# Attention over running maxima with the row sums in the value matmul, and its preparation with joint statistics

## The chip, the core and the metric

The kernel runs on one core of a Trainium2 chip. Its engines work side by side, each through its own list of instructions in order: TensorE (PE; PEld is its weight load), VectorE (DVE), ScalarE (ACT), GpSimd (POOL), and SyncE (SP), which issues the transfers. They meet at semaphores. The metric is the time of one execution on the device in microseconds.

## The reference

One inference step of a model of two layers, for 256 prompt tokens and 2048 latent tokens. Each layer projects the normalised input once into the inputs of four mixers (latent attention, a long convolution called Hyena, a state space called S5, gated linear attention called GLA), gates their outputs and projects them once back. The change touches the attention branch:

```
c_q = rmsnorm(c_q, p['mla_qa_norm'])
c_kv = rmsnorm(c_kv, p['mla_kva_norm'])
q = rmsnorm((c_q @ p['mla_w_uq']).reshape(b, L, MLA_HEADS, MLA_QK), p['mla_q_norm'])
k, v = mla_keys_values(c_kv, k_rope, p)
...
s = jnp.einsum('bqhd,bkhd->bhqk', qi, k).astype(jnp.float32) * (MLA_QK ** -0.5)
pr = jax.nn.softmax(s, axis=-1).astype(v.dtype)
return jnp.einsum('bhqk,bkhd->bqhd', pr, v)
```

There are 4 heads of 96 (64 of them from the latent, 32 rotary) with values of 64. A latent query reads 512 cached and 2048 latent keys; a prompt query reads the 256 prompt keys.

## The kernel before

Per layer the work runs in stages. First the input projection (`inproj`, its matmuls are in `mm3`, L268 to L270) with, beside it, S5 and the preparation of the attention (`mla_prep`). Then the attention for heads 0 and 1, with Hyena and GLA beside it. Then the attention for heads 2 and 3 with the output projection (L1817 to L1819). A scheduler that goes by priorities and by its own model of durations lays out each engine's list; the program text only gives the priorities.

`mla_prep` goes over 22 tiles of 128 tokens, 18 of this step and 4 cached. For a tile it computes the mean squares of c_q and c_kv, takes the inverse root with a helper of 13 VectorE instructions (`rsqrt`, an integer first guess and three Newton steps), scales, transposes, multiplies with the up-projections, takes a second inverse root for the 8 head vectors (4 of q, 4 of k), scales each, turns the rotary part on GpSimd (`rotate`), splits the result into two f16 halves (`split`) and stores it through a transposing transfer. Values are stored as high half in columns 0 to 63 and low half in 64 to 127.

`attention` goes over units, one head and one tile of 128 queries. A latent unit has three chunks of keys (1024, 1024 and 512), so there are 128 such units in the two layers, and 16 prompt units of one chunk. `scores` makes the scores of a chunk in PSUM in parts of 512 with three f16 matmuls each (L485 to L487), takes each part's row maximum (m, L488), the chunk's maximum (L492), from it the bias nb of the exponential (L493), and lets ScalarE write the exponentials e with their row sums su (L495). `values` splits e into f16 halves ph (L508 or L510, and L511 on GpSimd), turns them with a transposing transfer into pt (L513), and multiplies with V into one PSUM tile om (L517, L518). `combine` weighs the chunks against each other with al and the sums su, adds them up and writes the head's output o (L528 to L540). The scores of one chunk are issued ahead of the values of the chunk before. There is one buffer for om.

## Time and profile before

| | us |
|---|---|
| median of the 3 runs (lowest 4432.41, highest 4437.69) | 4437.48 |
| the profiled execution | 4438.93 |
| its span, first to last instruction | 4436.9 |
| TensorE busy in the span | 3680.0 |
| VectorE busy | 3222.7 |
| ScalarE busy | 2175.1 |
| GpSimd busy | 2048.8 |

Busy times are sums over the whole span; the stages differ, so what a change in one of them is worth is read from that stage. The mean granted clock of TensorE is 0.897 of its full speed.

### The profile page before, as it was taken

The numbers are of one execution on the slowest core, as the hardware profiler recorded it, in microseconds if no ns is written. First come the engines' busy times: TensorE is split into PE (matmuls) and PEld (weight loads), VectorE is DVE, ScalarE is ACT, GpSimd is POOL, SyncE is SP. The second block draws the span as 40 slices with busy tenths as digits, with TensorE's granted clock in tenths as the row PEclk, the third lists the DMA queues.
The fourth block names the chain that finished last, engine by engine and source line by source line (L and its number), as shares of the span: only waits on it lengthen the run. The fifth ranks groups of instructions, "written<-read, shape, count | busy, mean of one in ns | idle before, by whom it ended". The sixth has DMA issues, their size and how long they took to land. (4 is left out here: it accounts for less than half of the span.)

```text
span 4436.9 us, 67211 instructions
## 1 busy us (share of the span) xinstructions
PE 3680.0 (83%) x21852; PEld 2141.3 (48%) x21852; DVE 3222.7 (73%) x8340; ACT 2175.1 (49%) x4333; POOL 2048.8 (46%) x2025
## 2 busy tenths in 40 slices
PE   6899889787877887769887688889998888667898
PEld 2644545343555555424443554545565555434444
DVE  4775589984788887776786678866548887767774
ACT  3533334556545564675453344363435555545563
POOL 2553354741555654654453244424325555434553
PEclk7999999898777887989998899999998888887999
DMA  7746657656776788998988565633448776999886
GB/s 207 193 122 182 175 146 191 188 155 221 168 172 150 173 186 212 239 235 203 250 192 203 148 156 145 154 111 123 145 156 193 184 168 157 210 246 240 173 185 157
DMA packets 1343430, 799.91 MB, mean 180 GB/s; under 512 B 989588, under 2 KB 1221296, under 8 KB 1341544
## 3 DMA queue, kind: packets, MB, share of 16 engines
q1 hardware_dynamic: 1343080, 795.63, 71.8%
q8 instruction: 173, 2.83, 0.3%
q14 instruction: 177, 1.45, 0.1%
HBM read 352.12 MB, written 207.37 MB: 126 GB/s over the span
## 5 line engine op out<-in xcount | busy, mean ns | idle before, releaser
L511 POOL TENSOR_TENSOR ph<-e,ph 128x1024 f16<-128x1024 f32 (+2 forms) x400 | 725.5, 1821 | 650.4 <-ACT ph L508 323.9
L495 ACT ACTIVATE e<-sp,nb,ssc 128x512 f32<-128x512 f32 (+1 forms) x656 | 499.9, 767 | 415.7 <-DVE nb L493 347.0
L488 DVE TENSOR_REDUCE m<-sp 128x1 f32<-128x512 f32 (+1 forms) x656 | 438.0, 676 | 172.0 <-PE sp L487 170.2
L268 PE MATMUL mm<-hT,ws 128*128 128x512 f16 (+1 forms) x1440 | 526.5, 366 | 26.2 <-DVE wqh L75 13.3
L269 PE MATMUL mm<-hT,ws 128*128 128x512 f16 (+1 forms) x1440 | 526.4, 366 | 0.0
L270 PE MATMUL mm<-hT,ws 128*128 128x512 f16 (+1 forms) x1440 | 525.8, 365 | 0.0
L517 PE MATMUL om<-V,pt 128*128 128x128 f16 x2560 | 303.8, 235 | 132.1 <-DMA pt<-ph 90.6
L485 PE MATMUL sp<-KT,qt 128*128 128x512 f16 x640 | 271.5, 424 | 102.5 <-ACT e L495 99.1
L517 PEld LDWEIGHTS <-pt 128*128 128x128 f16 x2592 | 258.9, 109 | 171.6 <-DMA pt<-ph 125.1
L508 ACT CAST ph<-e 128x1024 f16<-128x1024 f32 (+2 forms) x268 | 269.0, 1004 | 117.3 <-DMA pt<-ph 115.2
L518 PE MATMUL om<-V,pt 128*128 128x64 f16 x2560 | 293.7, 206 | 0.0
L518 PEld LDWEIGHTS <-pt 128*128 128x128 f16 x2592 | 248.2, 105 | 71.6 <-issue 58.5
L486 PE MATMUL sp<-KT,qt 128*128 128x512 f16 x640 | 271.4, 424 | 0.0
L487 PE MATMUL sp<-KT,qt 128*128 128x512 f16 x640 | 268.9, 420 | 0.0
L1606 PE MATMUL lv<-qh,kh 32*128 32x128 f32 x1440 | 227.7, 324 | 25.1 <-DVE m L492 10.2
L1606 PEld LDWEIGHTS lv<-qh,kh 32*128 32x128 f32 x1440 | 188.0, 218 | 98.8 <-issue 30.3
L1817 PE MATMUL mm<-wo,bh 128*128 128x512 f16 x576 | 223.7, 389 | 7.7 <-DVE oy L1820 6.7
L268 PE MATMUL mm<-ws,hT 128*128 128x256 f16 (+1 forms) x864 | 215.4, 264 | 15.8 <-ACT z L1688 13.4
L269 PEld LDWEIGHTS <-ws 128*128 128x128 f16 x1440 | 143.8, 100 | 175.2 <-issue 49.4
L1818 PE MATMUL mm<-wo,bh 128*128 128x512 f16 x576 | 224.1, 389 | 4.2 <-DVE wo L1772 4.2
L1819 PE MATMUL mm<-wo,bh 128*128 128x512 f16 x576 | 223.9, 389 | 2.8 <-DVE bh L1792 2.8
L268 PEld LDWEIGHTS <-ws 128*128 128x128 f16 x1440 | 143.9, 100 | 150.9 <-issue 26.1
(522 smaller groups left out, 9489.1 us busy)
## 6 DMA issues: line engine op xcount, KB each, us to landing
kab<-KS SPq DMA_DIRECT2D x128, 256.0 KB
wf<-in_w_in SPq DMA_DIRECT2D x22, 1024.0 KB
b<-br SPq DMA_DIRECT2D x36, 512.0 KB
A1F<-a SPq DMA_DIRECT2D x64, 256.0 KB
zg<-z SPq DMA_DIRECT2D x64, 256.0 KB
...
```

The source lines that it names most:

```text
L268: nc.tensor.matmul(ps, lhsT=lh, rhs=rh, start=i == 0, stop=False)
L269: nc.tensor.matmul(ps, lhsT=lh, rhs=rl, start=False, stop=False)
L270: nc.tensor.matmul(ps, lhsT=ll, rhs=rh, start=False, stop=i == n - 1)
L485: nc.tensor.matmul(d, lhsT=qh, rhs=kh, start=True, stop=False)
L486: nc.tensor.matmul(d, lhsT=qh, rhs=kl, start=False, stop=False)
L488: nc.vector.tensor_reduce(m[:, 2 * c + i:2 * c + i + 1], d, axis=AX.X, op=ALU.max)
L495: nc.scalar.activation(e[:, i * 512:min(i * 512 + 512, n)], d, AF.Exp, bias=nb[:, c:c + 1], scale=ssc, accum_out=su[:, 2 * c + i:2 * c + i ...
L508: nc.scalar.copy(ph[:, 0:n], e)
L511: nc.gpsimd.tensor_tensor(out=ph[:, n:2 * n], in0=e, in1=ph[:, 0:n], op=ALU.subtract)
L517: nc.tensor.matmul(om[:, c], lhsT=pt[:, i], rhs=v, start=i == 0, stop=False)
L518: nc.tensor.matmul(om[:, c, 0:64], lhsT=pt[:, nk + i], rhs=v[:, 0:64], start=False, stop=i == nk - 1)
L1606: nc.tensor.matmul(ps[:, cc], lhsT=kh[hh, cc], rhs=qh[hh, cc], start=True, stop=True, tile_position=(32 * h, 0))
```

## The change

In the attention the chunk's maximum becomes a running one: the new L492 reduces over all parts so far, so the third bias is the smallest and no minimum has to be found. The bias itself (L493) is made on ScalarE. V gets a column of ones (a memset on GpSimd) and its halves change places, low first; the second matmul of each pair takes columns 64 to 128, so that column 128 of om collects the row sum from both halves of the exponentials, and the accumulator su goes. `combine` copies the first chunk out of om on ScalarE, adds the other two on VectorE, takes one reciprocal from column 128 and applies it in two steps, one on ScalarE and one on VectorE.

In the preparation the mean squares of c_q and c_kv are made when the input projection is evacuated (`tm` in `inproj`, into the tile zst that also holds the ones for `total`), and their inverse roots are taken for six tiles at once. q and k of a tile lie in one tile W of eight heads, copied there from PSUM by ScalarE; one square, one reduce, one inverse root, eight scalings, one rotation over eight heads. The two f16 tiles for the split are made once, with their zero columns. `rsqrt` itself takes 11 instructions, 8 where it has one column. A pad of 48 columns is added to the pool of K and V.

```diff
-    v = pool.tile([128, n], F32, tag=tag + "v", name=tag + "v")
     t = pool.tile([128, n], F32, tag=tag + "t", name=tag + "t")
     w = pool.tile([128, n], F32, tag=tag + "w", name=tag + "w")
-    nc.vector.tensor_scalar(out=v, in0=x, scalar1=mul, scalar2=EPS, op0=ALU.mult, op1=ALU.add)
-    nc.vector.tensor_single_scalar(out=t.bitcast(I32), in_=v.bitcast(I32), scalar=1, op=ALU.logical_shift_right)
-    nc.vector.tensor_scalar(out=out.bitcast(I32), in0=t.bitcast(I32), scalar1=-1.0, scalar2=float(0x5F3759DF),
-                            op0=ALU.mult, op1=ALU.add)
-    nc.vector.tensor_scalar(out=w, in0=v, scalar1=-0.5, scalar2=None, op0=ALU.mult)
+
+    nc.vector.tensor_scalar(out=w, in0=x, scalar1=-0.5 * mul, scalar2=-0.5 * EPS, op0=ALU.mult, op1=ALU.add)
+    nc.vector.tensor_scalar(out=out.bitcast(I32), in0=w.bitcast(I32), scalar1=-0.5,
+                            scalar2=float(0x5F3759DF - (1 << 30) - (1 << 22)), op0=ALU.mult, op1=ALU.add)
     for _ in range(3):
-        nc.vector.tensor_tensor(out=t, in0=out, in1=out, op=ALU.mult)
-        nc.vector.tensor_tensor(out=t, in0=t, in1=w, op=ALU.mult)
+        if n == 1:
+            nc.vector.scalar_tensor_tensor(out=t, in0=out, scalar=out, in1=w, op0=ALU.mult, op1=ALU.mult)
+        else:
+            nc.vector.tensor_tensor(out=t, in0=out, in1=out, op=ALU.mult)
+            nc.vector.tensor_tensor(out=t, in0=t, in1=w, op=ALU.mult)
         nc.vector.scalar_tensor_tensor(out=out, in0=t, scalar=1.5, in1=out, op0=ALU.add, op1=ALU.mult)
...
     def rotate(x, rope):
...
-        cs = rope[:, 0].unsqueeze(1).to_broadcast([128, 4, 32])
+        cs = rope[:, 0].unsqueeze(1).to_broadcast([128, 8, 32])
...
-    def split(x, dst, tag):
-
-        hl = tp.tile([128, NH, 2, 128], F16, tag=tag, name=tag, bufs=2)
+
+    hls = [tp.tile([128, NH, 2, 128], F16, name=f"hl{i}", bufs=1) for i in range(2)]
+    for hl in hls:
         nc.gpsimd.memset(hl[:, :, :, 96:128], 0.0)
+
+    def split(i, x, dst):
+
+        hl = hls[i]
         nc.scalar.copy(hl[:, :, 0, 0:96], x)
         nc.vector.tensor_tensor(out=hl[:, :, 1, 0:96], in0=x, in1=hl[:, :, 0, 0:96], op=ALU.subtract)
...
+    RS = 6
     for t in range(22):
         isctx = t >= 18
+        h0 = 4 if isctx else 0
         if not isctx:
+            if t % RS == 0:
+                rs = tp.tile([128, RS, 2], F32, tag="rs", name="rs", bufs=2)
+                rsqrt(s, tp, rs.rearrange("p t c -> p (t c)"), s.zst[:, t:t + RS].rearrange("p t c -> p (t c)"), 1.0, 2 * RS, "cr")
             z = tp.tile([128, 384], F32, tag="z", name="z", bufs=2)
             nc.sync.dma_start(z, s.zm[l][t * 128:(t + 1) * 128])
             kr = z[:, 320:352]
             if t < 16:
                 rope = tp.tile([128, 2, 32], F32, tag="rope", name="rope", bufs=2)
                 nc.sync.dma_start(rope, I["k_rope"][:, t])
-            st = tp.tile([128, 2], F32, tag="st", name="st")
-            rs = tp.tile([128, 2], F32, tag="rs", name="rs")
-            cn = tp.tile([128, 320], F32, tag="cn", name="cn")
-            nc.scalar.activation(cn[:, 0:192], z[:, 0:192], AF.Square, scale=192 ** -0.5, accum_out=st[:, 0:1])
-            nc.scalar.activation(cn[:, 192:320], z[:, 192:320], AF.Square, scale=128 ** -0.5, accum_out=st[:, 1:2])
-            rsqrt(s, tp, rs, st, 1.0, 2, "cr")
-            nc.vector.scalar_tensor_tensor(out=cn[:, 0:192], in0=z[:, 0:192], scalar=rs[:, 0:1], in1=qa, op0=ALU.mult, op1=ALU.mult)
-            nc.vector.scalar_tensor_tensor(out=cn[:, 192:320], in0=z[:, 192:320], scalar=rs[:, 1:2], in1=kva, op0=ALU.mult, op1=ALU.mult)
+            cn = tp.tile([128, 320], F32, tag="cn", name="cn", bufs=2)
+            nc.vector.scalar_tensor_tensor(out=cn[:, 0:192], in0=z[:, 0:192], scalar=rs[:, t % RS, 0:1], in1=qa, op0=ALU.mult, op1=ALU.mult)
+            nc.vector.scalar_tensor_tensor(out=cn[:, 192:320], in0=z[:, 192:320], scalar=rs[:, t % RS, 1:2], in1=kva, op0=ALU.mult, op1=ALU.mult)
             ckv = cn[:, 192:320]
...
+        W = tp.tile([128, 8, 96], F32, tag="qk", name="qk", bufs=2)
+        ct = tp.tile([128, 3, 128], F32, tag="ct", name="ct", bufs=2)
...
+        nc.scalar.copy(W[:, 4:8, 0:64], kv[:, :, 0:64])
+        nc.scalar.copy(W[:, 4:8, 64:96], kr.unsqueeze(1).to_broadcast([128, 4, 32]))
...
-            nc.scalar.activation(q2[:, 0:384], qp, AF.Square)
-            nc.vector.tensor_reduce(ss[:, 0:4], q2[:, 0:384].rearrange("p (h n) -> p h n", h=4), axis=AX.X, op=ALU.add)
-            rsqrt(s, tp, rr, ss, 1.0 / QK, 8, "qr")
-            q = tp.tile([128, 4, 96], F32, tag="qk", name="q")
-            for h in range(4):
-                nc.vector.scalar_tensor_tensor(out=q[:, h], in0=qp[:, h * 96:(h + 1) * 96], scalar=rr[:, h:h + 1], in1=qn,
-                                               op0=ALU.mult, op1=ALU.mult)
-            if t < 16:
-                rotate(q, rope)
-            split(q, s.QT[l][t].rearrange("p h a t -> p (h a) t"), "hl")
...
-        k = tp.tile([128, 4, 96], F32, tag="qk", name="k")
-        for h in range(4):
-            nc.vector.scalar_tensor_tensor(out=k[:, h, 0:64], in0=kv[:, h, 0:64], scalar=rr[:, 4 + h:5 + h], in1=kn[:, 0:64],
-                                           op0=ALU.mult, op1=ALU.mult)
...
+            nc.scalar.copy(W[:, 0:4], qp.rearrange("p (h n) -> p h n", h=4))
...
+        nh = 8 - h0
+        ss = tp.tile([128, nh], F32, tag=f"ss{nh}", name="ss", bufs=2)
+        rr = tp.tile([128, nh], F32, tag=f"rr{nh}", name="rr", bufs=2)
+        sq = tp.tile([128, 768], F32, tag="sq", name="sq", bufs=1).rearrange("p (h n) -> p h n", h=8)[:, h0:]
+        nc.scalar.activation(sq, W[:, h0:], AF.Square)
+        nc.vector.tensor_reduce(ss, sq, axis=AX.X, op=ALU.add)
+        rsqrt(s, tp, rr, ss, 1.0 / QK, nh, f"qr{nh}")
+        for h in range(h0, 8):
+            nc.vector.scalar_tensor_tensor(out=W[:, h], in0=W[:, h], scalar=rr[:, h - h0:h - h0 + 1], in1=qn if h < 4 else kn,
                                            op0=ALU.mult, op1=ALU.mult)
         if t < 16:
-            rotate(k, rope)
-        split(k, s.KT[l].rearrange("p h a t -> p (h a) t")[:, :, kt * 128:(kt + 1) * 128], "hl")
+            rotate(W, rope)
...
+            V = kp.tile([128, (b - a) // 128, 130], F16, tag="V" + nm, name="V" + nm)
             nc.sync.dma_start(K, s.KT[l][:, h, :, a:b])
-            nc.sync.dma_start(V, s.V[l][h, :, a // 128:b // 128])
+            nc.gpsimd.memset(V[:, :, 128:129], 1.0)
+            nc.sync.dma_start(V[:, :, 0:128], s.V[l][h, :, a // 128:b // 128])
...
-        mc = m[:, 2 * c:2 * c + 1]
-        if len(sps) > 1:
-            nc.vector.tensor_tensor(out=mc, in0=mc, in1=m[:, 2 * c + 1:2 * c + 2], op=ALU.max)
-        nc.vector.tensor_scalar(out=nb[:, c:c + 1], in0=mc, scalar1=nssc, scalar2=LN2_15, op0=ALU.mult, op1=ALU.add)
+        mc, k = m[:, 0:1], 2 * c + len(sps)
+        if k > 1:
+            mc = m[:, 5 + c:6 + c]
+            nc.vector.tensor_reduce(mc, m[:, 0:k], axis=AX.X, op=ALU.max)
+        nc.scalar.activation(nb[:, c:c + 1], mc, AF.Copy, scale=nssc, bias=LN2_15)
         for i, d in enumerate(sps):
-            nc.scalar.activation(e[:, i * 512:min(i * 512 + 512, n)], d, AF.Exp, bias=nb[:, c:c + 1], scale=ssc,
-                                 accum_out=su[:, 2 * c + i:2 * c + i + 1])
+            nc.scalar.activation(e[:, i * 512:min(i * 512 + 512, n)], d, AF.Exp, bias=nb[:, c:c + 1], scale=ssc)
...
-            nc.tensor.matmul(om[:, c], lhsT=pt[:, i], rhs=v, start=i == 0, stop=False)
-            nc.tensor.matmul(om[:, c, 0:64], lhsT=pt[:, nk + i], rhs=v[:, 0:64], start=False, stop=i == nk - 1)
+            nc.tensor.matmul(om[:, c], lhsT=pt[:, i], rhs=v[:, 0:129], start=i == 0, stop=False)
+            nc.tensor.matmul(om[:, c, 64:129], lhsT=pt[:, nk + i], rhs=v[:, 64:129], start=False, stop=i == nk - 1)
 
     def combine(u, C):
-        nb, su, om = u["nb"], u["su"], u["om"]
-        al, dn, mx = small(4, "al"), small(1, "dn"), small(1, "mx")
-        w = tp.tile([128, 128], F32, tag="wo", name="wo")
-        sc = su.rearrange("p (c i) -> p c i", i=2)
-        last = C - 1
+        nb, om = u["nb"], u["om"]
+        al, dn = nb[:, 3:5], nb[:, 5:6]
+        w = tp.tile([128, 129], F32, tag="wo", name="wo")
         if C > 1:
 
-            nc.vector.tensor_reduce(mx, nb[:, 0:C], axis=AX.X, op=ALU.min)
-            nc.scalar.activation(al[:, 0:C], nb[:, 0:C], AF.Exp, bias=mx, scale=-1.0)
-            nc.vector.tensor_tensor(out=sc[:, 0:C], in0=sc[:, 0:C], in1=al[:, 0:C].unsqueeze(2).to_broadcast([128, C, 2]), op=ALU.mult)
-            nc.vector.tensor_reduce(dn, su[:, 0:u["ns"]], axis=AX.X, op=ALU.add)
-            nc.vector.reciprocal(dn, dn)
-            nc.vector.tensor_scalar(out=al[:, 0:C], in0=al[:, 0:C], scalar1=dn, scalar2=None, op0=ALU.mult)
+            nc.scalar.activation(al, nb[:, 0:2], AF.Exp, bias=nb[:, 2:3], scale=-1.0)
+            nc.scalar.activation(w, om[:, 0], AF.Copy, scale=al[:, 0:1])
+            nc.vector.scalar_tensor_tensor(out=w, in0=om[:, 1], scalar=al[:, 1:2], in1=w, op0=ALU.mult, op1=ALU.add)
+            nc.vector.tensor_tensor(out=w, in0=om[:, 2], in1=w, op=ALU.add)
         else:
-            nc.vector.reciprocal(al[:, 0:1], su[:, 0:1])
-        nc.vector.tensor_scalar(out=w, in0=om[:, last], scalar1=al[:, last:C], scalar2=None, op0=ALU.mult)
-        for c in range(last):
-            nc.vector.scalar_tensor_tensor(out=w, in0=om[:, c], scalar=al[:, c:c + 1], in1=w, op0=ALU.mult, op1=ALU.add)
+            nc.scalar.copy(w, om[:, 0])
+        nc.vector.reciprocal(dn, w[:, 128:129])
+        nc.scalar.activation(w[:, 0:64], w[:, 0:64], AF.Copy, scale=dn)
         o = pairs[u["h"] // 2, u["t"]][1]
-        nc.vector.tensor_tensor(out=o[:, u["h"] % 2 * 64:u["h"] % 2 * 64 + 64], in0=w[:, 0:64], in1=w[:, 64:128], op=ALU.add)
+        nc.vector.scalar_tensor_tensor(out=o[:, u["h"] % 2 * 64:u["h"] % 2 * 64 + 64], in0=w[:, 64:128], scalar=dn, in1=w[:, 0:64],
+                                       op0=ALU.mult, op1=ALU.add)
...
+            if ms is not None:
+                junk = z[0][:, 384:512].bitcast(F16)
+                nc.scalar.activation(junk[:, 0:192], z[0][:, 0:192], AF.Square, scale=192 ** -0.5, accum_out=ms[:, t, 0:1])
+                nc.scalar.activation(junk[:, 0:128], z[0][:, 192:320], AF.Square, scale=128 ** -0.5, accum_out=ms[:, t, 1:2])
...
+            kp.tile([128, PADK], F32, name="pad", bufs=1)
```

How the lists change, at the places that the prediction speaks of. VectorE (DVE) in the attention of the second layer, before: where one latent unit is combined and its row sums are scaled (su, dn, al are the sums, the reciprocal and the weights; wo is the combined row, o the output).

```order
L536 TENSOR_SCALAR wo<-om,al 128x128 [waits PE_49]
L528 TENSOR_REDUCE mx<-nb 128x1 [waits DVE_49]
L538 SCALAR_TENSOR_TENSOR wo<-om,al,wo 128x128 [waits DVE_49] x2
L540 TENSOR_TENSOR o<-wo 128x64 [waits DVE_49]
L895 TENSOR_TENSOR y<-y,xs 128x512 [waits Pool_49]
L510 CAST ph<-e 128x512 [waits DMAHW6_49,Activation_49]
L530 TENSOR_TENSOR su<-su,al 128x6 [waits Activation_49]
L531 TENSOR_REDUCE dn<-su 128x1 [waits DVE_49]
```

The same engine and stage after the change, again at the combine of a latent unit (nb now also holds the reciprocal and the weights).

```order
L527 SCALAR_TENSOR_TENSOR wo<-om,nb,wo 128x129 [waits Activation_49]
L528 TENSOR_TENSOR wo<-om,wo 128x129 [waits DVE_49]
L531 RECIPROCAL nb<-wo 128x1 [waits DVE_49]
L487 TENSOR_REDUCE m<-sp 128x1 [waits PE_49] x2
L492 TENSOR_REDUCE m<-m 128x1 [waits DVE_49]
L886 TENSOR_TENSOR y<-h,kab 128x512 [waits DMAHW7_49,DMAHW4_49,Activation_49]
L534 SCALAR_TENSOR_TENSOR o<-wo,nb 128x64 [waits Activation_49]
```

The scaling of the sums and of the weights has left VectorE, and its first and its last step of the combine now wait for ScalarE.

ScalarE (ACT) in the first layer, beside the output projection, before (L1787, L1791 and L228 belong to that projection; L508 is the cast of e to f16).

```order
L495 ACTIVATE e,su<-sp,nb,ssc_7567 128x512 [waits DVE_49]
L495 ACTIVATE e,su<-sp,nb,ssc_7567 128x512
L1787 ACTIVATE bh,bss<-b 128x1024 [waits DMAHW2_49,PE_49]
L495 ACTIVATE e,su<-sp,nb,ssc_7567 128x512 [waits DVE_49]
L508 CAST ph<-e 128x1024 [waits DMAHW6_49,Activation_49]
L529 ACTIVATE al<-nb,mx 128x3 [waits DVE_49]
L1791 ACTIVATE bh<-b,bps 128x1024 [waits DVE_49,Activation_49]
```

The same engine and stage after the change (L526 copies the first chunk out of om, L532 applies the reciprocal).

```order
L526 ACTIVATE wo<-om,nb 128x129 [waits PE_49]
L222 ACTIVATE hl,hq<-oy 128x1024 [waits DMAHW0_49,DVE_49,Pool_49]
L493 ACTIVATE nb<-m,nssc_7578 128x1 [waits DVE_49]
L532 ACTIVATE wo<-wo,nb 128x64 [waits DVE_49]
L495 ACTIVATE e<-sp,nb,ssc_7576 128x512 [waits Activation_49]
L495 ACTIVATE e<-sp,nb,ssc_7576 128x512
L493 ACTIVATE nb<-m,nssc_7578 128x1 [waits DVE_49]
L1788 ACTIVATE bh<-b,bps 128x1024 [waits DVE_49]
L507 CAST ph<-e 128x1024 [waits DMAHW3_49,Activation_49]
```

The wait for VectorE's maximum has moved from the exponential to nb in front of it, and two more instructions of the combine stand in ScalarE's list, one waiting for TensorE and one for VectorE.

## Rows read from the trace of the kernel before

**Rows 1.** Windows: length; PE, PEld, DVE, ACT, POOL busy; clock; DMA share; GB/s.
```profile
500.00:1080.00 580.00, 489.94 (x2370) 255.95 (x2369) 475.43 (x1404) 288.52 (x629) 273.38 (x393) 0.92 0.61 168
1080.00:1700.00 620.00, 501.95 (x3389) 341.70 (x3388) 507.80 (x1178) 325.17 (x677) 348.27 (x311) 0.82 0.77 179
1700.00:2480.00 780.00, 605.36 (x3482) 316.94 (x3482) 557.14 (x1344) 423.43 (x761) 365.06 (x227) 0.90 0.89 220
2480.00:3300.00 820.00, 736.64 (x4403) 435.81 (x4401) 558.94 (x1779) 338.57 (x726) 307.65 (x498) 0.96 0.50 134
3300.00:3750.00 450.00, 384.91 (x2511) 259.59 (x2510) 361.21 (x858) 245.20 (x507) 253.61 (x220) 0.84 0.77 181
3750.00:4100.00 350.00, 242.16 (x1517) 146.03 (x1518) 246.80 (x567) 190.94 (x370) 153.08 (x95) 0.82 0.95 231
4100.00:4437.00 337.00, 298.39 (x2056) 158.79 (x2054) 222.33 (x582) 164.56 (x326) 160.60 (x101) 0.96 0.77 172
```
**Rows 2.** Waits, whole span: engine and line, releaser: us in total, times, longest.
```profile
ACT e L495 <- DVE nb L493: 347.0, 141, 9.2
```
**Rows 3.** Timeline, first layer's attention: start us, us, engine, line, operation, shapes.
```profile
1116.61 2.88 POOL L1596 TENSOR_TENSOR att<-quad,ws 128x1536 f32<-128x1536 f32 x1
...
1117.38 2.12 DVE L492 TENSOR_TENSOR m<-m 128x1 f32<-128x1 f32 x1
```
**Rows 4.** Single lines: duration in ns as min/median/max, first and last start.
```profile
L492 DVE TENSOR_TENSOR m<-m x256: 136/157/2298, 1106.8 to 4345.2; 128x1 f32<-128x1 f32 x128
...
L511 POOL TENSOR_TENSOR ph<-e,ph x400: 667/2125/4166, 1112.5 to 4378.7; 128x1024 f16<-128x1024 f32 x93, 128x512 f16<-128x512 f32 x35, 128x256 f16<-128x256 f32 x6
```
**Rows 5.** Groups of VectorE, whole span: count | busy us, mean ns | idle before.
```profile
L492 DVE TENSOR_TENSOR m<-m 128x1 f32<-128x1 f32 x256 | 129.0, 504 | 1.1
...
L538 DVE SCALAR_TENSOR_TENSOR wo<-om,al,wo 128x128 f32<-128x128 f32 x256 | 88.0, 344 | 2.3
...
L533 DVE TENSOR_SCALAR al<-al,dn 128x3 f32<-128x3 f32 x128 | 83.3, 651 | 1.2
...
L493 DVE TENSOR_SCALAR nb<-m,nssc 128x1 f32<-128x1 f32 x400 | 76.3, 205 | 2.1
...
L530 DVE TENSOR_TENSOR su<-su,al 128x6 f32<-128x6 f32 x128 | 62.1, 485 | 18.6 <-ACT e L495 14.7 <-ACT al L529 3.6
...
L536 DVE TENSOR_SCALAR wo<-om,al 128x128 f32<-128x128 f32 x144 | 49.3, 342 | 48.0 <-PE om L518 47.7
...
L528 DVE TENSOR_REDUCE mx<-nb 128x1 f32<-128x3 f32 x128 | 19.2, 150 | 2.0
```
**Rows 6.** Groups of ScalarE, whole span.
```profile
L495 ACT ACTIVATION_READ_ACCUMULATOR e<-sp,nb,ssc 128x1 f32 x656 | 128.7, 196 | 0.0
...
L529 ACT ACTIVATE al<-nb,mx 128x3 f32<-128x3 f32 x128 | 37.7, 295 | 12.4 <-DVE mx L528 12.1
...
L1688 ACT ACTIVATE z<-mm,wun 128x256 f32<-128x256 f32 x72 | 33.8, 470 | 59.0 <-PE mm L270 51.7 <-issue 2.8 <-DMA zqk<-z 2.1
```
**Rows 7.** The page's line on DMA packets.
```profile
DMA packets 1343430, 799.91 MB, mean 180 GB/s; under 512 B 989588, under 2 KB 1221296, under 8 KB 1341544
```
**Rows 8.** Chain from 3300 us by line; first and last of L533's 24 pieces.
```profile
by line: DMA pt<-ph 12.3%; DVE m L488 6.8%; issue 5.8%; PE lv L1606 5.0%; ACT e L495 4.6%; DVE m L492 3.4%; SPq L513 3.1%; POOL ph L511 2.6%; PE om L517 2.4%; PE sp L485 2.3%; PE h L931 2.2%; PE h L936 2.1%; PE sp L486 2.0%; PE sp L487 1.9%
...
3343.84 0.14 DVE al L533
...
4342.37 0.53 DVE al L533
```
**Rows 9.** Groups of VectorE from 500 to 1080 us.
```profile
L448 DVE SCALAR_TENSOR_TENSOR k<-z,rr,row 128x32 f32<-128x32 f32 x72 | 23.4, 325 | 0.0
...
L63 DVE TENSOR_TENSOR crt<-rs 128x2 f32<-128x2 f32 x54 | 11.7, 218 | 0.5
...
L64 DVE TENSOR_TENSOR crt<-crt,crw 128x2 f32<-128x2 f32 x54 | 11.1, 205 | 0.5
L65 DVE SCALAR_TENSOR_TENSOR rs<-crt,rs 128x2 f32<-128x2 f32 x54 | 10.9, 202 | 0.3
```

More of the change, by code (lines that the diff above doesn't have):

```diff
@@ new lines, in mla_prep @@
+        kt = t + 4 if t < 18 else t - 18
+        vd = tp.tile([128, NH, 128], F16, tag="vd", name="vd", bufs=2)
+        nc.scalar.activation(vd[:, :, 64:128], kv[:, :, 64:128], AF.Copy, scale=sv)
+        nc.vector.scalar_tensor_tensor(out=vd[:, :, 0:64], in0=kv[:, :, 64:128], scalar=sv, in1=vd[:, :, 64:128],
+                                       op0=ALU.mult, op1=ALU.subtract)
+        nc.sync.dma_start(s.V[l][:, :, kt].rearrange("h p d -> p h d"), vd)
+        nh = 8 - h0
+        ss = tp.tile([128, nh], F32, tag=f"ss{nh}", name="ss", bufs=2)
@@ L476, in scores @@
         e = tp.tile([128, 1024], F32, tag="e", name="e", bufs=3)[:, 0:n]
-        nb, su, m = u["nb"], u["su"], u["m"]
-        parts = range(0, n, 512)
+        nb, m = u["nb"], u["m"]
         sps = []
-        for i, a in enumerate(parts):
+        for i, a in enumerate(range(0, n, 512)):
             w = min(512, n - a)
@@ L502, in values @@
         if first:
[L503 removed]
+            u["om"] = ps_o.tile([128, 3, 129], F32, tag="om", name="om")
         om = u["om"]
@@ L1417, in gla_decays @@
     V.memset(one, 1.0)
-    gw = tp.tile([32, 2, 128], F32, tag="cn", name="gw")
+    gw = tp.tile([32, 2, 128], F32, tag="cn", name="gw", bufs=2)
     G.memset(gw, 0.0)
@@ L1681, in to, with tm @@
         return evac
-    def tm(dst, c0, n, last=True):
+    def tm(dst, c0, n, last=True, ms=None):
         def evac(t, ps, un):
```

52 lines of the change are left out of this document (17 added, 35 removed).

## The prediction, made before the changed kernel ran

> **What bounds the kernel now.** I read the stages first, then who waits for whom, then the duration spread of the small VectorE operations, then the chain that ended last. In [rows 1] the preparation of the first layer is the second of 500 to 1080 us, its attention fills 1080 to 2480, the second layer's preparation 2480 to 3300, its attention 3300 to 4437. No engine is full in the attention: TensorE is busy 81% of 1080 to 1700 at a granted clock of 0.82, VectorE 82%; from 3750 to 4100 TensorE 69% at 0.82 and VectorE 71%, while the DMA engines are at 0.95. At 4100 to 4437 TensorE is 89% busy at 0.96. So the attention is a ring of engines that wait for each other, with VectorE and TensorE alike near the top, a DMA limit in two of its stages, and TensorE itself near its limit only at the end and in 2480 to 3300 (90%).
>
> The longest wait of the whole program is that of the exponential (ACT, L495) for the bias nb that VectorE makes: 347.0 us in 141 waits [rows 2]. Why VectorE is late shows in [rows 3]: the maximum of two single columns, L492, takes 2.12 us, and it ends when the GpSimd operation that began 0.77 us before it ends. In [rows 4] the same instruction has a median of 157 ns and a maximum of 2298; its mean is 504 [rows 5], and the GpSimd subtraction beside it has a median of 2125. So operations of one to six elements that read SBUF on VectorE cost three times their own work, because they stand behind GpSimd. The reduces do not: L528, over three columns, averages 150 ns [rows 5].
>
> **The change, part by part.** *Attention.* A latent unit (128 of them) loses two L492, three L493, L530, L531, L533, L528 and L536 on VectorE. By [rows 5]: 129.0 + 76.3 + 62.1 + 83.3 + 19.2 + 49.3, and another 19.2 for L531, which is L528's like: 438 us. It gains three reduces over two to five columns, 384 at L528's 150 ns, 58 us. Of the two L538 one stays and one becomes a tensor_tensor with the same PSUM and SBUF operands, taken as even; the last addition L540 becomes another operation with two SBUF inputs, also even. Net 380 us of the 1895 us of VectorE in the attention stages [rows 1], 20%.
>
> ScalarE gets what left: 400 nb, 144 copies out of PSUM (129 columns) and 144 scalings of 64 columns. The nearest rows are L529 with three columns, 295 ns, and L1688 with 256 columns out of PSUM, 470 ns [rows 6]. 400 x 0.295 + 144 x 0.38 + 144 x 0.33 (the last two between the ends, being nearer L529) = 220 us; the 656 accumulator reads go, 128.7 us [rows 6]. Net 91 us on an engine that is busy 1349 of 2537 us there [rows 1], so 53% becomes 57%: no bound.
>
> TensorE: 2560 pairs of matmuls grow by one column each; against 128 and 64 columns that is nothing that a row can show, and I take 0. V is now loaded in pieces of 256 B, 20 a partition: eight loads of 2560 packets, 20,480 on 1.34 million [rows 7], 1.5%. They are issued a head ahead, beside the scores of the head before, so 0; uncovered, once a layer, they could cost some microseconds.
>
> What this is worth on the path: from 3300 on, the chain holds L492 with 3.4% of 1137 us, 39 us, and L533 with 24 pieces, together 20.0 us [rows 8]. Leaving 150/504 of L492's share for the new reduces, 47 us per layer go; the smaller removed pieces and the ScalarE instructions in their place I estimate as even. Two layers: 95 us. That is the lower bound if the order stays and another path does not take over. From the other side, if half of the 380 us comes back, as between two engines that take turns, 190. I take 140, and both ends for the range.
>
> *Preparation.* A token tile loses the per-tile inverse root for its two norms. Three of that chain's lines, with 54 pieces each, are 33.7 us in the first layer [rows 9]; now three such chains serve 18 tiles, a sixth, 6 us. Counting instructions per tile, 46 on VectorE become 27 (13 of the small chain become 2, 13 of the large one 11, twelve scalings 8, two reduces and an addition one reduce): 19 x 18 tiles at about 0.2 us [rows 9] is 69 us, less some 10 for the longer reduce: about 60 us a layer. In 500 to 1080 VectorE is busy 475 of 580 us [rows 1]; I count half, 30 us, as path. In the second layer TensorE is busy 737 of 820 us, so a quarter, 15. ScalarE's added copies there lie beside TensorE's projection, which sets the end of both stages; without that cover they are some 1 us a tile.
>
> There is one step against the change. The eight scalings per tile now read W and the weight row both from SBUF, where before most read PSUM. L448, which read SBUF twice, has a mean of 325 ns for 32 columns [rows 9]; so I credit the fall from twelve to eight but no faster instruction.
>
> The Trainium skill, "Advanced Engine Details and Errata", VectorE Performance Modes, Mode Summary, says that VectorE's second SBUF port is shared with GpSimd and that the two block each other. The trace agrees: one column, 2.12 us [rows 3]. By that rule the eight scalings stand behind GpSimd as well: if they cost as much as the twelve did, 4 x 18 scalings at L448's 0.325 us, 23 us a layer, drop out, 60 becomes 37, and the sum 167 instead of 185.
>
> The Trainium skill, "DMA: Bandwidth & Descriptors", Specifications, asks for at least 512 B a transfer for full rate; V's new 256 B pieces are below it. No row here prices that, and the sum has 0 for it.
>
> Sum: 140 + 30 + 15 = 185. The profiled execution took 4438.9 us, 2.0 more than its span and 1.4 more than the median of the runs; 4438.9 - 185 - 1.4 = 4252, and I say 4255.
>
> **Rivals.**
> *The hand-overs on ScalarE make it slower.* The combine used to go TensorE, then VectorE to the end. Now ScalarE copies om (waits for TensorE), VectorE adds, ScalarE scales (waits for VectorE's reciprocal), VectorE ends. The ACT rows above show what stands behind: the exponentials of the next chunks, for which TensorE's next scores wait, and the one PSUM tile om is not free until ScalarE's turn has come. Price: 288 new waits; if they wait as often and as long as nb does, 141 of 400 and 2.46 us each [rows 2], 250 us. If all of it came onto the path: 4252 + 250, about 4500. It decides from three quarters, 185 us, on. Against it: ScalarE is idle 47% there.
>
> *DMA and TensorE hold the attention.* From 1700 to 2480 and 3750 to 4437 the DMA share is 0.77 to 0.95 and the transposes alone are 12.3% of the chain [rows 1, 8]. Then only 1080 to 1700 and 3300 to 3750 give, say half of the chain's 95 us, and the preparation 45: 4437 - 93, about 4345.
>
> *VectorE was the bound throughout.* If every attention stage rose to the 89% of TensorE that the last one has, its 2033 busy us over 2537 [rows 1] would need 2284, a gain of 253; with all 60 and a quarter of the preparation, 75: about 4110.
>
> *The saving goes idle.* The scheduler lays out every queue anew, and chance in it eats the rest: no change.
>
> **How the numbers follow.** The forecast (about 4200 to 4310) 0.48; held by DMA 0.24; VectorE the bound 0.14; idle 0.04; slower 0.10. The range 4120 to 4400 leaves out the slower case, the idle case and the far end of the gain, some 2 in 10. A difference below 0.2%, 9 us, could not be told from none. Faster 0.86, same 0.04, slower 0.10.
>
> **What would show it.** Right: VectorE's busy time down by some 480 to 520 us, the mean of the new L492 reduce near 150 ns with no tail, the wait of ACT for VectorE (now at L493) well below 347 us, the clock in 1080 to 1700 above 0.82, VectorE in 500 to 1080 below its 475 us. Wrong: ACT waiting for long at L526 and L532, TensorE at its first value matmul for VectorE's last read of om; the scalings L444 with a mean far above 325 ns; or VectorE's busy time down as said and the attention as long as before, with the DMA share at 0.95 in more stages.

## The result and the profile after

The changed kernel takes 4309.8 us (median of 4 runs, 4306.7 to 4312.8), the kernel before 4434.9 (4 runs); the ratio is 0.973, 95% interval 0.9693 to 0.9767: faster by 125 us at the medians. The forecast was 4255, so the time lies 55 us above it. The profiled execution took 4312.8 us with a span of 4311.0.

The page after, busy time by engine ([rows 1] give the stages of before; the page of before has DVE 3222.7 and ACT 2175.1):

```profile
PE 3613.2 (84%) x21852; PEld 2101.6 (49%) x21852; DVE 2909.4 (67%) x6406; ACT 2313.6 (54%) x4363; POOL 2023.8 (47%) x1837
```

VectorE is down by 313 us where 480 to 520 were foreseen, ScalarE is up by 138. The stages below run from mark to mark: the first score matmul of each layer, and the first projection matmul of the second layer. Single lines of TensorE in both traces (the projection by its weight loads; duration in ns as min/median/max, first and last start), the kernel before first, then the changed kernel:

```profile
L485 PE MATMUL sp<-KT,qt x320: 376/379/634, 1104.1 to 2357.3; 128*128 128x512 f16 x160
...
L268 PEld LDWEIGHTS <-hT x432: 95/98/291, 2466.1 to 2915.4; 128*128 128x128 f16 x144
...
L485 PE MATMUL sp<-KT,qt x320: 376/379/634, 3326.3 to 4341.4; 128*128 128x512 f16 x160
```

```profile
L484 PE MATMUL sp<-KT,qt x320: 376/379/634, 1115.7 to 2267.5; 128*128 128x512 f16 x160
...
L271 PEld LDWEIGHTS <-hT x432: 95/98/291, 2385.3 to 2822.4; 128*128 128x128 f16 x144
...
L484 PE MATMUL sp<-KT,qt x320: 376/379/634, 3239.1 to 4205.0; 128*128 128x512 f16 x160
```

So the first layer's attention begins 12 us later (1104.1, 1115.7), lasts until the second layer's projection 1362 us before and 1270 after, the projection 860 and 854, the rest 1104 and 1065. The whole gain lies in the two attention stages, 92 and 39 us; the stages that hold the preparation give nothing on balance (12 us later, 6 shorter). The windows of these stages, the kernel before and then the changed one (columns as in [rows 1]):

```profile
0.00:1104.00 1104.00, 927.96 (x4649) 491.83 (x4650) 780.34 (x2065) 499.67 (x992) 468.21 (x585) 0.92 0.64 178
1104.00:2466.00 1362.00, 1077.41 (x6612) 638.79 (x6611) 1046.85 (x2470) 729.69 (x1404) 702.76 (x525) 0.86 0.84 199
2466.00:3326.00 860.00, 774.96 (x4665) 464.87 (x4666) 578.59 (x1833) 358.25 (x763) 318.73 (x514) 0.96 0.51 139
3326.00:4437.00 1111.00, 899.63 (x5932) 545.84 (x5931) 816.92 (x1974) 587.49 (x1176) 559.06 (x402) 0.87 0.83 191
```

```profile
500.00:1080.00 580.00, 506.67 (x2603) 266.93 (x2602) 468.59 (x1103) 293.51 (x570) 280.22 (x324) 0.94 0.62 171
1080.00:1700.00 620.00, 507.99 (x3490) 338.30 (x3488) 460.28 (x962) 402.02 (x762) 359.38 (x310) 0.89 0.86 200
0.00:1116.00 1116.00, 960.21 (x4919) 515.85 (x4920) 778.80 (x1759) 520.88 (x1017) 486.31 (x530) 0.93 0.64 178
1116.00:2385.00 1269.00, 998.71 (x6339) 585.75 (x6337) 871.66 (x1768) 776.48 (x1394) 680.75 (x487) 0.89 0.90 212
2385.00:3239.00 854.00, 794.71 (x4674) 474.25 (x4675) 538.57 (x1450) 375.11 (x766) 290.41 (x417) 0.94 0.51 140
3239.00:4311.00 1072.00, 859.52 (x5923) 525.72 (x5921) 720.37 (x1431) 641.16 (x1188) 566.35 (x404) 0.90 0.87 198
```

Over 1080 to 1700 the changed kernel's clock is 0.89, against 0.82 in [rows 1], and VectorE in 500 to 1080 is busy 468.6 us against 475.4: two of the signs that the prediction named, the second by 7 us only. VectorE's share of the first attention fell from 77% (1046.85 of 1362) to 69%, the DMA share rose from 0.84 to 0.90. Before the first score VectorE is as busy as ever, 780 and 779 us, although it runs 306 instructions fewer.

**Where VectorE's saving went.** Groups of VectorE after (count | busy us, mean ns | idle before), then their counterparts before:

```profile
L509 DVE CAST ph<-e 128x512 f16<-128x512 f32 (+1 forms) x132 | 145.2, 1100 | 72.8 <-DMA pt<-ph 54.8 <-ACT e L495 17.6 <-ACT ph L507 0.2
...
L534 DVE SCALAR_TENSOR_TENSOR o<-wo,nb 128x64 f32<-128x64 f32 x144 | 99.6, 692 | 57.8 <-ACT wo L532 57.4
...
L444 DVE SCALAR_TENSOR_TENSOR qk<-qk,rr,row 128x96 f32<-128x96 f32 x320 | 83.4, 330 | 0.8
L887 DVE TENSOR_TENSOR y<-y,xs 128x512 f32<-128x512 f32 x64 | 81.9, 1279 | 4.8 <-POOL xs L885 4.5
...
L492 DVE TENSOR_REDUCE m<-m 128x1 f32<-128x2 f32 (+2 forms) x384 | 55.0, 147 | 1.9
```

```profile
L510 DVE CAST ph<-e 128x512 f16<-128x512 f32 (+1 forms) x132 | 87.4, 662 | 75.7 <-DMA pt<-ph 47.3 <-ACT e L495 25.1 <-POOL ph L511 1.6
...
L540 DVE TENSOR_TENSOR o<-wo 128x64 f32<-128x64 f32 x144 | 67.4, 468 | 1.3
...
L895 DVE TENSOR_TENSOR y<-y,xs 128x512 f32<-128x512 f32 x64 | 56.6, 884 | 2.8 <-POOL xs L893 2.5
```

The new reduce L492 is as foreseen, 147 ns and no tail. But the cast of e, the last addition of the combine and a product of the Hyena filter, whose outputs have the same shapes as before, cost 327 us after and 211 before: 115 us came back there, some 10 of them because L534 does more than L540 did (median 286 against 220 ns).

That the rest is standing behind GpSimd shows in the single records. Of the records longer than one and a half medians, all 97 of L492 before end 0.01 to 0.02 us after the end of a GpSimd operation that was already running or began within 0.03 us of their start; after the change so do all 62 of L534 (by up to 0.09 us), all 56 of the cast and all 31 of the product (by up to 0.55 us, less than their own median). The work of [rows 4] that holds VectorE up most, L511 on GpSimd (now L510), is as long as it was (1821 ns a time before, 1843 after). So stalls were taken off L492 and L533, and other operations now have more of them. The bias nb never had any: L493 before has a median of 202 ns and a maximum of 424, so "three times their own work" in the prediction holds for L492, L530 and L533, not for all small operations. The Trainium skill, "SBUF — State Buffer", SBUF: two separate sides, calls the pair of ports an exclusive lock that one of the two engines holds for a whole instruction; the trace agrees, since L534 has a median of 286 ns and a maximum of 2368 in this line:

```profile
L534 DVE SCALAR_TENSOR_TENSOR o<-wo,nb x144: 269/286/2368, 1152.6 to 4261.5; 128x64 f32<-128x64 f32 x144
```

**Who waits.** Waits of ScalarE, VectorE and TensorE after (total us, times, longest):

```profile
ACT nb L493 <- DVE m L492: 254.0, 164, 7.0
...
PEld L516 <- DMA pt<-ph: 156.1, 97, 5.8
...
PE om L516 <- DMA pt<-ph: 117.0, 76, 5.4
...
ACT wo L526 <- PE om L517: 68.7, 40, 6.0
...
DVE o L534 <- ACT wo L532: 57.4, 53, 3.6
...
DVE wo L527 <- ACT wo L526: 44.3, 43, 4.5
...
ACT wo L532 <- DVE nb L531: 31.3, 29, 3.5
```

The wait of [rows 2] became 254.0. The new hand-overs of the combine are there, 68.7 + 57.4 + 44.3 + 31.3 us. TensorE's matmuls of the values wait longer than before for the transposed e (117.0 and 90.6, its weight loads 156.1 and 125.1), and for five windows of 100 us in the first attention the DMA share is above 1 (in the same windows before it is 0.80 to 0.98):

```profile
1600.00:1700.00 100.00, 74.63 (x348) 41.17 (x346) 60.46 (x108) 67.80 (x117) 45.86 (x34) 0.89 1.02 254
1700.00:1800.00 100.00, 80.61 (x448) 43.39 (x447) 64.59 (x122) 81.27 (x139) 61.40 (x43) 0.95 1.05 244
1800.00:1900.00 100.00, 78.60 (x487) 44.06 (x487) 68.95 (x122) 70.79 (x125) 62.86 (x40) 0.97 1.06 258
1900.00:2000.00 100.00, 64.87 (x334) 31.67 (x335) 47.01 (x90) 52.53 (x83) 27.46 (x15) 0.80 1.01 265
2000.00:2100.00 100.00, 88.97 (x542) 46.17 (x541) 65.75 (x145) 55.16 (x97) 49.16 (x27) 0.95 1.04 242
```

### The profile page after: what moved, and what is told of

Read it like the earlier page. It is cut to its first block, busy times and chain, and to the rows that moved or that the text cites. A ratio compares the mean times of both kernels' runs of the same rounds, so it can differ in the third digit from the quotient of the medians.

```text
span 4311.0 us, 65111 instructions
## 1 busy us (share of the span) xinstructions
PE 3613.2 (84%) x21852; PEld 2101.6 (49%) x21852; DVE 2909.4 (67%) x6406; ACT 2313.6 (54%) x4363; POOL 2023.8 (47%) x1837
## 5 line engine op out<-in xcount | busy, mean ns | idle before, releaser
L510 POOL TENSOR_TENSOR ph<-e,ph 128x1024 f16<-128x1024 f32 (+2 forms) x400 | 735.7, 1843 | 537.6 <-ACT ph L507 267.3
L495 ACT ACTIVATE e<-sp,nb,ssc 128x512 f32<-128x512 f32 (+1 forms) x656 | 474.7, 768 | 18.2 <-POOL ph L510 7.9
L516 PE MATMUL om<-V,pt 128*128 128x129 f16 x2560 | 308.0, 237 | 148.0 <-DMA pt<-ph 113.0
L516 PEld LDWEIGHTS <-pt 128*128 128x128 f16 x2592 | 263.1, 107 | 201.1 <-DMA pt<-ph 156.1
L484 PE MATMUL sp<-KT,qt 128*128 128x512 f16 x640 | 263.6, 412 | 84.2 <-ACT e L495 78.8
L517 PE MATMUL om<-V,pt 128*128 128x65 f16 x2560 | 298.3, 206 | 0.0
L517 PEld LDWEIGHTS <-pt 128*128 128x128 f16 x2592 | 254.7, 105 | 58.8 <-issue 46.5
L485 PE MATMUL sp<-KT,qt 128*128 128x512 f16 x640 | 263.2, 411 | 0.0
L486 PE MATMUL sp<-KT,qt 128*128 128x512 f16 x640 | 261.9, 409 | 0.0
L493 ACT ACTIVATE nb<-m,nssc 128x1 f32<-128x1 f32 x400 | 113.1, 291 | 262.3 <-DVE m L492 254.0
L272 PEld LDWEIGHTS <-ws 128*128 128x128 f16 x1440 | 144.0, 100 | 177.6 <-issue 53.2
L271 PEld LDWEIGHTS <-ws 128*128 128x128 f16 x1440 | 144.6, 100 | 153.3 <-issue 29.1
L273 PEld LDWEIGHTS <-ws 128*128 128x128 f16 x1440 | 144.2, 100 | 149.4 <-issue 26.2
```

The costliest lines, as they stand in the source:

```text
L271: nc.tensor.matmul(ps, lhsT=lh, rhs=rh, start=i == 0, stop=False)
L272: nc.tensor.matmul(ps, lhsT=lh, rhs=rl, start=False, stop=False)
L273: nc.tensor.matmul(ps, lhsT=ll, rhs=rh, start=False, stop=i == n - 1)
L495: nc.scalar.activation(e[:, i * 512:min(i * 512 + 512, n)], d, AF.Exp, bias=nb[:, c:c + 1], scale=ssc)
L510: nc.gpsimd.tensor_tensor(out=ph[:, n:2 * n], in0=e, in1=ph[:, 0:n], op=ALU.subtract)
L516: nc.tensor.matmul(om[:, c], lhsT=pt[:, i], rhs=v[:, 0:129], start=i == 0, stop=False)
```

## The experiments

Every time is a median, every ratio one to the kernel before on the same chip, with its 95% interval.

| run | us | ratio | to first score | first attention | projection | second attention |
|---|---|---|---|---|---|---|
| before | 4434.9 | 1 | 1104 | 1362 | 860 | 1104 |
| changed | 4309.8 | 0.973 (0.9693 to 0.9767) | 1116 | 1270 | 854 | 1065 |
| attn_only | 4303.9 | 0.972 (0.9687 to 0.9752) | 1108 | 1259 | 868 | 1055 |
| prep_only | 4392.5 | 0.9926 (0.9903 to 0.9949) | 1115 | 1317 | 855 | 1101 |
| reduce_max | 4427.0 | 0.9996 (0.9972 to 1.0019) | 1106 | 1335 | 861 | 1118 |
| nb_on_dve | 4377.6 | 0.989 (0.9862 to 0.9917) | 1116 | 1305 | 852 | 1095 |
| after_pad0 | 4366.3 | 0.9864 (0.9825 to 0.9904) | 1117 | 1322 | 857 | 1056 |
| after_pad96 | 4776.5 | 1.079 (1.0751 to 1.083) | 1092 | 1477 | 850 | 1358 |
| before_pad24 | 4427.8 | 0.9999 (0.9971 to 1.0028) | 1109 | 1352 | 860 | 1091 |
| before_pad48 | 4863.4 | 1.0984 (1.0944 to 1.1024) | 1083 | 1545 | 866 | 1362 |
| nb_on_dve_held | 4329.1 | 0.9773 (0.9749 to 0.9798) | 1114 | 1284 | 848 | 1076 |
| combine_on_dve_held | 4313.8 | 0.974 (0.9714 to 0.9765) | 1119 | 1267 | 846 | 1060 |
| reduce_max_held | 4388.8 | 0.9902 (0.9874 to 0.9931) | 1106 | 1342 | 863 | 1077 |
| reduce_nb_act_held | 4377.2 | 0.9888 (0.9864 to 0.9913) | 1103 | 1345 | 860 | 1076 |

The four columns on the right are worked out from first starts in each trace, as the marks above, and end at the start of the last matmul of the output projection; they belong to one execution, and the kernel before ranged over 4402 to 4455 us, so a column tells some 20 us.

**The two parts apart.** attn_only is the kernel before with the attention, the pad and V's order of halves:

```
-        nc.scalar.activation(vd[:, :, 0:64], kv[:, :, 64:128], AF.Copy, scale=sv)
+        nc.scalar.activation(vd[:, :, 64:128], kv[:, :, 64:128], AF.Copy, scale=sv)
...
+            kp.tile([128, PADK], F32, name="pad", bufs=1)
```

> The attention part alone (its functions, V's order of halves and the pad of the kv pool), with the preparation and the inverse root of the kernel before. Theory A, from the stage marks of the two traces (first score matmul of layer 0: 1104.5 before, 1116.5 after; first projection matmul of layer 1: 2466.4 and 2385.6; first score matmul of layer 1: 3326.7 and 3239.5): the attention part carries all of the 125 us, the preparation nothing. Then this kernel takes 4300 to 4325 us. Theory B, that of the prediction: the preparation is worth 45 us by itself, and the attention therefore only 80: 4355. Theory C, the layout of the queues by the scheduler is worth more than either: anything from 4280 to 4400, with stage marks that differ from those of the changed kernel by more than 20 us in both directions.

prep_only is the changed kernel with those lines and the attention taken back.

> The preparation part alone (new inverse root, joint statistics of the norms, eight heads together), with the attention of the kernel before. Theory A: no gain, 4425 to 4450 us, the first score matmul of layer 0 between 1100 and 1120 and VectorE busy in 500 to 1100 within 15 us of the 485 us of before, since the eight scalings and the longer square and reduce take what the shorter chains leave. Theory B: 4390, VectorE's busy time there down by 60. Theory C: up to 40 us to either side.

The attention part alone, which includes the pad, carries the whole gain, 124 us by the medians. The preparation alone gives 0.74%, 33 us: theory A was wrong that it gives nothing. Theory B, right in the time, was wrong in the place: VectorE in 500 to 1100 is busy 475.4 us against 485.4, not 60 less. In prep_only too the first score is 11 us later than before; the gain stands in the attention behind it. Why is seen in two lines of the DMA queue, the store of the prepared K and the first load of v of the gated linear attention (GLA). The kernel before:

```profile
L373 SPq DMA_DIRECT2D KT<-xt x22: 524/552/727, 570.8 to 988.8; - x22
...
L1488 SPq DMA_DIRECT2D v<-zv x12: 370/410/538, 1050.8 to 1521.4; - x12
```

The changed kernel:

```profile
L380 SPq DMA_DIRECT2D KT<-xt x22: 534/559/1327, 563.4 to 812.9; - x22
...
L1480 SPq DMA_DIRECT2D v<-zv x12: 370/408/1537, 906.7 to 1374.2; - x12
```

The preparation itself ends 176 us earlier (988.8, 812.9), more than the 30 us foreseen. But the attention can't use it: its K is first loaded as the projection ends, at 1074.2 and 1083.2 (rows at the end), the last projection matmul standing at 1064.1 and 1084.8; in SyncE's queue these loads stand among and behind the projection's last stores. What does use it is GLA, which starts 144 us earlier; with it 270 matmuls (4919 against 4649 before the first score) and some 93 us of other VectorE work move from the attention into the preparation's stage and fill the time that was freed. With the attention of before, those matmuls are missed there: 1362 to 1317. With the new attention they are not: 1259 us with 6613 matmuls in attn_only, 1270 with 6339 in the changed kernel. The two gains, 124 and 33, don't add up. That the matmuls which moved are what shortens the stage is argued from these counts, not shown; nor was the preparation run with the order held, so how much of its 33 us is order stays open.

**One line of the change.** reduce_max is the kernel before with

```
-            nc.vector.tensor_tensor(out=mc, in0=mc, in1=m[:, 2 * c + 1:2 * c + 2], op=ALU.max)
+            mc = m[:, 5 + c:6 + c]
+            nc.vector.tensor_reduce(mc, m[:, 2 * c:2 * c + 2], axis=AX.X, op=ALU.max)
```

> The kernel before with one edit: the maximum of the two halves of a chunk is a reduce over the two columns in place of a tensor_tensor of two single columns. Nothing else moves. VectorE loses the tail of that operation (256 times 504 ns to 256 times some 150 ns, 90 us of busy time). Theory A, the stalls are on the path: the 39 us that the chain of before held on this line fall by two thirds in each layer, some 50 us in both, 4385. Theory D, the stall is only handed on to the next VectorE operation that needs the shared port (the maxima's bias L493, the cast of ph, the combine): then L493's mean rises from 191 ns, the sum of busy time falls by less than 45 us, and the time is within 15 us of before, 4420 to 4440.

nb_on_dve is the changed kernel with

```
-        nc.scalar.activation(nb[:, c:c + 1], mc, AF.Copy, scale=nssc, bias=LN2_15)
+        nc.vector.tensor_scalar(out=nb[:, c:c + 1], in0=mc, scalar1=nssc, scalar2=LN2_15, op0=ALU.mult, op1=ALU.add)
```

> The changed kernel with the bias nb made on VectorE again, as before; the running maxima stay. Theory A: the two-port operation of one column comes back into the chain between scores and exponential, 400 times with a tail up to 2 us; the wait of ACT for VectorE grows again from 254 us towards 347, and the time by 20 to 40 us, 4330 to 4350. Rival E, the hand-over to ScalarE costs as much as the stall did (294 ns on ScalarE against 191 on VectorE): no change, 4300 to 4320. Rival F, ScalarE is now what is waited for: faster, under 4300.

Both are odd. The removal of 90 us of stalls is worth nothing; theory D has the time right, and VectorE's busy time fell by 44 us (3178.8), just under its 45, but nb's mean stayed (206 ns, 205 before). And a move that leaves VectorE's busy time nearly alone (2947 against 2909 us) costs 68 us, more than any theory had. Theory A's way to it did not come: nb on VectorE has a maximum of 223 ns and no tail, and ScalarE waits 203 us for it, less than the 254. Each edit also makes the scheduler lay out all queues anew, so the next four aim at that alone.

**The order.** The pad ahead of the kv pool computes nothing. after_pad0 takes its line out, after_pad96 doubles it, the other two put it into the kernel before:

```
-            kp.tile([128, PADK], F32, name="pad", bufs=1)
```

> The changed kernel without the pad of 48 columns ahead of the kv pool. Nothing that is computed moves; tiles lie at other addresses, so what a new tile has to wait for, and with it the order that the scheduler gives every queue, is another. Theory A, the gain comes from the work that left VectorE: 4295 to 4330, as with the pad. Theory C, a good part of it is the order that this pad happened to give, as the 68 us between this kernel and the one with nb on VectorE would then be as well: 4340 to 4400.

> The changed kernel with a pad of 96 columns instead of 48, a third order of the same work. Theory A: 4295 to 4330. Theory C: far from the other two pads, the three spread over 40 us or more.

> The kernel before with the changed kernel's pad of 48 columns ahead of the kv pool, and nothing else. Theory A: 4410 to 4445, no change. Theory C: the pad alone moves it by 20 to 60 us to either side.

> The kernel before with a pad of 24 columns, a third order of that kernel's work. Theory A: 4410 to 4445. Theory C: the three orders of the kernel before spread over 40 us or more, and the 35 us of the preparation by itself are no more than such a step.

Theory C is right about the pad: the same work takes 4310, 4366 or 4776 us, and that of before 4432, 4428 or 4863 (with 24 columns, as theory A had it; with 48, far beyond the 20 to 60 us of theory C). Without a pad in either kernel the gain is 65 us (4366 against 4432). The large step has a visible place, in both layers: 207 us of it lie in after_pad96's first attention, 293 in the second. GLA's loads of v in after_pad96, first and second layer, and the GpSimd products of the Hyena filter in the first:

```profile
L1480 SPq DMA_DIRECT2D v<-zv x12: 370/373/561, 1729.3 to 2109.8; - x12
...
L1480 SPq DMA_DIRECT2D v<-zv x12: 359/376/496, 4050.2 to 4310.5; - x12
```

```profile
L1018 POOL TENSOR_TENSOR hv<-hv,hx x10: 1265/2348/2844, 1383.0 to 1705.0; 128x1024 f32<-128x1024 f32 x8, 128x512 f32<-128x512 f32 x2
```

GLA now starts at 1729 instead of 907, after the Hyena filter instead of beside it (1736 in before_pad48). In the second layer it is the same: 4050 instead of 3026, after the filter's last product at 4037 (before_pad48 has 4125, before 3127). Windows of after_pad96:

```profile
1100.00:1300.00 200.00, 135.56 (x1013) 82.17 (x1014) 115.18 (x239) 143.49 (x261) 105.69 (x65) 0.92 1.02 214
1300.00:1500.00 200.00, 149.07 (x1074) 87.10 (x1072) 120.61 (x249) 139.12 (x267) 104.68 (x69) 0.91 0.96 214
1500.00:1700.00 200.00, 130.89 (x815) 80.95 (x816) 113.48 (x205) 109.52 (x202) 90.48 (x55) 0.84 0.99 233
...
2100.00:2300.00 200.00, 146.99 (x669) 106.78 (x669) 101.33 (x238) 50.56 (x91) 65.37 (x74) 0.66 0.26 84
...
4100.00:4300.00 200.00, 153.58 (x772) 138.69 (x773) 118.81 (x268) 37.49 (x82) 89.17 (x115) 0.52 0.11 35
```

The transfers of the filter and of the attention lie beside each other at a DMA share of 0.96 to 1.02, and afterwards GLA runs with the DMA engines at 0.26 and TensorE at a granted clock of 0.66, in the second layer at 0.11 and 0.52. Which tile GLA had to wait for was not traced. The small step, 56 us between no pad and 48 columns, lies in the first attention (1322, 1270); GLA starts alike in both (905.2, 906.7), and its cause stays open.

**The same edits with the order held.** In the last four kernels every engine issues in the order that the scheduler gave the reference kernel; an instruction that changes its engine keeps its place in time.

```
+    for k, i in sorted(((at[T0[j]], i) for j, i in enumerate(L) if ...
+        e = str(i.engine)
+        if e in last:
+            tc.add_manual_dep(i, last[e], mybir.DependencyInfo(mybir.DependencyClass.NoSync, ...
+        last[e] = i.name
```

nb_on_dve_held has nb_on_dve's edit, reduce_max_held that of reduce_max, reduce_nb_act_held that and nb on ScalarE in the kernel before. combine_on_dve_held has

```
-            nc.scalar.activation(w, om[:, 0], AF.Copy, scale=al[:, 0:1])
+            nc.vector.tensor_scalar(out=w, in0=om[:, 0], scalar1=al[:, 0:1], scalar2=None, op0=ALU.mult)
...
-        nc.scalar.activation(w[:, 0:64], w[:, 0:64], AF.Copy, scale=dn)
+        nc.vector.tensor_scalar(out=w[:, 0:64], in0=w[:, 0:64], scalar1=dn, scalar2=None, op0=ALU.mult)
```

> The changed kernel with the bias nb on VectorE again, and every engine held to the order that the scheduler gave the changed kernel (nb stands in VectorE's queue where it stood in time in ScalarE's). TensorE, GpSimd and the DMA queue issue exactly what they issue in the changed kernel. With the order free this edit cost 68 us. Theory G, those 68 us were a new order: 4300 to 4325 us, within 15 of the changed kernel. Theory A, they are the work itself, 400 operations back in the chain between scores and exponential: 4355 to 4390. Between, the two have a share each.

> The changed kernel with the three ScalarE steps of the combine (copy with the first weight, plain copy of a prompt unit, scaling of 64 columns) on VectorE, every engine held to the order of the changed kernel. It takes away two hand-overs a unit, whose waits in the changed kernel are 68.7 + 44.3 + 57.4 + 31.3 us, and puts some 0.34 + 0.3 us a unit back on VectorE, 144 units, 90 us of busy time. Theory A, VectorE's queue is what the attention waits for: slower, 4325 to 4360. The prediction's slower rival, the hand-overs cost: faster, 4250 to 4295. Theory G, neither is on the path in this order: 4300 to 4325.

> The kernel before with the maximum of two columns as a reduce, every engine held to the order of the kernel before; 256 instructions of VectorE are another operation and nothing else is different. With the order free the time was the same, 4427. Theory A, the tail of this line is on the path (the chain of before held 39 us of it in the second layer): 4370 to 4400. Theory D, the stall is handed on to the next operation that shares the port: 4415 to 4440.

> The kernel before with that reduce and with nb on ScalarE, every engine held to the order of the kernel before: VectorE loses the tail of L492 (90 us of busy time) and L493 (76 us), ScalarE gains 400 times 0.29 us, 116. Theory A: the two together are most of what the attention part gained, 4340 to 4380. Theory G, with the order of before held nothing comes of it, since the gain of the changed kernel lies in the order that the scheduler could choose: 4410 to 4440. Rival E, ScalarE's longer queue costs more than VectorE's shorter one gives: over 4440.

With the order held the picture is orderly. (No run held the order with no edit; that combine_on_dve_held stays within 4 us of the changed kernel speaks for the holding costing nothing.) The reduce alone is worth 0.98%, 31 to 56 us by its interval, 35 by the medians; theory A's 4370 to 4400 holds, and D falls: VectorE's busy time is down by 79 of the 92 us that its line lost.

```profile
PE 3658.5 (83%) x21852; PEld 2128.1 (48%) x21852; DVE 3143.7 (72%) x8340; ACT 2177.1 (50%) x4333; POOL 2041.8 (46%) x2025
```

```profile
L494 DVE TENSOR_REDUCE m<-m 128x1 f32<-128x2 f32 x256 | 36.8, 144 | 1.1
```

nb costs 19 us when it goes back (its interval just overlaps the changed kernel's) and gives 12 when it moves in the order of before (not to be told from 0); of the 68 us some 50 were order. The reduce and nb together, 47 us by the medians, reach theory A's range (4377) but are not most of the attention's 124. The combine on VectorE changes nothing, 4314 against 4310, although two hand-overs a unit are gone and VectorE is busy 85 us longer; the run doesn't tell whether neither counts or the two cancel:

```profile
PE 3601.2 (84%) x21852; PEld 2095.2 (49%) x21852; DVE 2994.4 (70%) x6694; ACT 2240.4 (52%) x4075; POOL 2028.0 (47%) x1837
```

## Why the forecast was right in sign and 55 us too far

- **The attention term, 140.** Alone it is 124, in the changed kernel 92 + 39 = 131 by the marks: the size was near, in part by luck: without a pad in either kernel the whole change gives 65. Its best step was the chain's share of L492, 39 us a layer of which 27 should go ([rows 8] and the reduce's 150 ns): with the order held the second attention lost 27 us and the first 21, columns that tell some 20 us. The step "the smaller removed pieces and the ScalarE instructions in their place are even" was near enough for nb (12 to 19 us) and for the combine's ScalarE steps against VectorE's (0 within 10). The rest of the 124, some 75 us, was not taken apart, L533's 20 us a layer not either: after_pad0, 56 us above the changed kernel, says that most of it can come from the order.
- **The preparation term, 30 + 15.** This is the step that failed. It took half and a quarter of VectorE's saved time as path. The saving was larger than the 60 us a layer: VectorE's own instructions of the preparation fell by 94 us in the first layer and by 80 in the second, summed over their groups. On balance none of it was path in its own stages: with this part the first score comes 5 to 16 us later (1114 to 1119 in six kernels, against 1103 to 1109 in six without it; the two with GLA behind the filter are left out), and the second projection is shorter by 3 to 22 us. TensorE's projection ends both stages, as the prediction said of ScalarE's copies but not of VectorE's chain: in the first layer K's last store lies 75 us ahead of the last projection matmul already in the kernel before, and 272 us in the changed one. What the part gave, 33 us by itself and nothing beside the new attention, came by GLA's earlier start or by the order.
- **VectorE's busy time, down by 480 to 520.** It fell by 313. The forecast added up durations of single records, and neighbouring records overlap: below, L492 starts 0.08 us before the record ahead of it ends, and the next starts as far before L492 ends (start us, us).

```profile
4005.66 0.68 DVE L487 TENSOR_REDUCE m<-sp 128x1 f32<-128x512 f32 x1
4006.26 0.14 DVE L492 TENSOR_REDUCE m<-m 128x1 f32<-128x2 f32 x1
4006.32 0.15 DVE L1787 TENSOR_TENSOR bun<-bpi,woi 128x1 f32<-128x1 f32 x1
```

  Summed over all records of each trace the durations fell by 439 us (3712.8 to 3274.1); busy time counts an overlap once, and 1934 records fewer took 126 us of overlaps with them. The 439 are the removed lines less the new reduce, 383, and the preparation's 174, less what came back. The 438 us of removed lines were priced with their stalls ([rows 3, 4]); a stall belongs to the GpSimd work, which stayed, and part of it moved to other operations that meet that work. With the order held and one line changed, 13 of 92 us were handed on; over the whole change, 115 us on three lines.
- **Not in the sum: the pad and the order.** The line PADK of the change was left out; the order stood only in the idle rival, at 0.04 and as something that could eat the gain. The pad decides 56 us of the 125 in the changed kernel, and 430 or more with other values.
- **The slower rival, ScalarE's hand-overs.** The waits came, 202 us of them, and the 250 us of the rival did not: trading them for 85 us of VectorE work changes nothing.
- **DMA and TensorE hold the attention.** Speaks for it: the share of 1.01 to 1.06 over 500 us, longer waits for the transposes, and that 273 matmuls fewer in the first attention no longer help. So does where the lead is won: 40% of the first layer's value matmuls are done at 1620 us before and 1540 after, 60% at 1880 and 1811, all at 2376 and 2289, so a lead of 80 us is won before the share passes 1, and at the end it is 87. The product of share and length is 1144 us before, 1142 after and 1133 in attn_only; by these three, an estimate, the stage, now 1270, would come to some 1140 if the share were 1 throughout. No run changed the transfers alone; this is argued, not shown.
- **L444's scalings, the step against the change.** Median 314 ns for 96 columns, mean 330 ([rows 9] had 325 for L448's 32): no faster instruction, as credited. Only 9 of 320 records are longer than one and a half medians, so the stalls that the prediction priced at 23 us a layer are not there; the sentence cited beside that price speaks of VectorE operations that use two ports. By the sum of durations the scalings fell from 147 us to 106.
